# Attention scores as 64-row float32 product pairs, and another order of the input projections, in a two-layer hybrid block

## The chip, the cores and the metric

One core of one Trainium2 chip runs the whole two-layer block in one launch. The metric is the time of the launch on the device in microseconds; the median of the runs shown counts. The text names the engines as the profile does: PE multiplies matrices (PEld is its weight loading), DVE, ACT and POOL work element by element, SP issues the transfers.

## The reference

For 256 tokens of width 1024, each of two layers does `x = x + rms_norm(mixer(rms_norm(x)))` and then `x = x + rms_norm(swiglu(rms_norm(x)))`, all in float32. The mixer multiplies the normed input by a weight of 1024 x 6484 and cuts the product into the inputs of four branches:

```
ssm   (br 0): conv of xs, bs, cs (4 taps, silu), gate z, state-space scan, 8 heads
fox   (br 1): softmax(q k^T / 8 + cf_q - cf_k) v, causal, 8 heads of 64
moba  (br 2): softmax(rope(q) rope(k)^T / 8) v, causal (256 tokens are one block), 8 heads
dsa   (br 3): the same, over the 64 keys per query with the largest index score
              sum_h w_h relu(rope(iq_h) . rope(ik)), 4 index heads
out = (sum_n sigmoid(h Wg_n + b) * (y_n Wb_n)) Wo
```

## The kernel before

A weight matrix is worked off in **pieces**. A chunk of 1 MB is loaded by SP (three buffers, `raw`), and each half of it is split into a rounded part `whi` (ACT, line 307) and a rest `wlo` (DVE, line 123), 128x1024 each. A piece of a projection then is 24 PE matmuls of 256 columns: `hh*whi`, `hl*whi`, `hh*wlo` over 8 blocks of the input width (`emit_b`), where `hh` and `hl` are the split of the normed input. The splits run ahead of PE by constants: `HA = 3` pieces for `whi`, `LA = 2` for `wlo`. Some pieces (`mv`, `fv`, `dv`, the output projections) are 12 matmuls of 512 columns instead.

All other work is written as generators, and one step of each active one is emitted per **turn** (`tick`). The main loop emits, for each piece: the loads and splits ahead, the piece's matmuls, then one turn. Every engine executes in the order of emission. In a turn come first the `posts` (what follows a piece's matmuls, such as `rope_post`, `conv_post`, `z_post`), then the active generators, and then, if `STEP` turns have gone by since the last one, the next **unit** is taken from the list `units`. A unit is one pair of heads: `attn_gen` for the branches fox, moba and dsa (four units each), or `ssd_gen` for ssm (four). So there are 16 units per layer, in the order in which their projections are done. Here `STEP` is 3. `index_gen` computes the index scores (line 813), and then the top keys in 16 turns of a maximum and a replacement (lines 820 and 821), and sets the flag for which the dsa units wait.

A layer's mixer has 51 pieces of input projection in the order mv 4, fv 4, small 1, iq 2, mq 4, mk 4, xs 4, bs 2, cs 2, z 4, fq 4, fk 4, dv 4, dq 4, dk 4 (numbered 0 to 50 here). Then come four blocks of 12 pieces, one for each branch in the order 2, 0, 1, 3: in each, twice, four gate pieces and two projections of the branch's output `y`. The first projections are pieces 55, 67, 79 and 91. Before a projection `drain` gives further turns, with no piece between them, until the branch's last unit has set its flag.

An attention unit takes 14 turns: one for `split_k` (line 776 on ACT, 779 on DVE, 780 on POOL), one for `split_q` (764 on ACT, 767 on DVE), one to spare, then the steps score, low, expo, recip, norm, tr, ev for its two heads, one turn apart, then the product with v (`pv_mms`, all of 128 rows and 64 output columns, the two heads on separate halves of the columns), its rounding and its rest. The split puts the rounded q and its rest on top of each other as 128 rows, and k twice, so that `s_mms` gets a head's scores from one 128-row matmul with k's rounded part and one with k's rest (in zero-padded tiles `klz`), for each of two query tiles: 128 queries by 128 keys and 128 queries by 256 keys. Fox adds a third with the decay row (`csS`).

Of the kernel before, what the change touches and what calls it, by code (L numbers as in the profile page):

```python
# [15 lines left out]
P = 128  # L16
# [24 lines left out]
def host_constants():  # L41
    import numpy as np
    c = np.zeros((P, NCST), np.float32)
    p = np.arange(P)
    l = np.arange(S)
    c[:, C_ID:C_ID + P] = np.eye(P, dtype=np.float32)
    c[:, C_TRI:C_TRI + P] = p[:, None] <= p[None, :]
    c[:, C_ONE:C_ONE + P] = 1.0
    c[:, C_MASK:C_MASK + P] = np.where(p[None, :] > p[:, None], BIG, 0.0)
    c[:, C_MASK + P:C_MASK + 3 * P] = np.where(l[None, :] > p[:, None] + P, BIG, 0.0)  # L50
    c[:, C_MASKT:C_MASKT + P] = np.where(p[None, :] < p[:, None], -BIG, 0.0)
    inv = np.power(np.float32(10000.0), -np.arange(0, 64, 2, dtype=np.float32) / np.float32(64)).astype(np.float32)
    ang = (np.arange(S, dtype=np.float32)[:, None] * inv[None, :]).astype(np.float32)
    j = (p % 64) // 2
    c[:, C_COS:C_COS + S] = np.cos(ang).astype(np.float32)[:, j].T
    c[:, C_SIN:C_SIN + S] = np.sin(ang).astype(np.float32)[:, j].T * np.where(p % 2 == 0, -1.0, 1.0)[:, None]
    for r in range(16):
        c[r, C_SEL + r] = 1.0
        c[32 + r, C_SEL + r] = 1.0
    return c  # L60
# [2 lines left out]
NS4 = 26  # L63
TAIL = 6
MID = 1
STEP = 3
HA = 3
LA = 2

# [22 lines left out]
def kernel(ctx: ExitStack, tc: tile.TileContext, a, out):  # L92
# [68 lines left out]
    nh = cp.tile([P, 1], F32, name="nh")  # L161
    V.memset(nh, -0.5)
    csS = cp.tile([P, S], F32R, name="csS")
    klz = [cp.tile([P, 2, S], F32R, name=f"klz{i}") for i in range(2)]
    turn = [0]
    par = cp.tile([P, DEPTH, 76], F32, name="par")
    av = cp.tile([P, DEPTH, 16], F32, name="av")
    dsk = cp.tile([P, DEPTH, 4], F32, name="dsk")
# [13 lines left out]

    def clear_pads():
        G.memset(csS.bitcast(F32), 0.0)
        for z in klz:
            G.memset(z.bitcast(F32), 0.0)

    def setup_params():
        V.tensor_copy(sel, cst[:, C_SEL:C_SEL + 16])
        pp = aps()  # L190
        for l in range(DEPTH):
            T.transpose(pp[:, l * P:(l + 1) * P], rows[:, l, :], ident)
        pv = pp[:, 0:2 * P].rearrange("p (l c) -> p l c", l=DEPTH)
        V.tensor_scalar(par[:, :, 0:72], pv[:, :, 0:72], 0.5, None, op0=ALU.mult)
        V.tensor_copy(par[:, :, 72:76], pv[:, :, 72:76])
        V.memset(av, -1.0)
        for l in range(DEPTH):
            ea = tp.tile([P, 8], F32, name="ea")
            A.activation(ea, hd[:, l, 2, :], AF.Exp)
            V.tensor_scalar(av[:, l, 0:8], ea, -1.0, None, op0=ALU.mult)  # L200
            V.tensor_copy(dsk[0:64, l, :], hd[0:64, l, 3, 0:8:2])
            V.tensor_copy(dsk[64:128, l, :], hd[64:128, l, 3, 1:8:2])
# [309 lines left out]
    def mixer(l):  # L512
# [81 lines left out]
        def z_post(base):  # L594
            def f(j, o):
                i = base + j
                if i == 0:
                    L["sz"] = big("sz")
                zh = t1k("zh")
                A.activation(zh, o, AF.Copy, scale=0.5)  # L600
                yield from silu_half(zh, L["sz"][:, i, :])
                if i == 3:
                    L["y", 0] = (big("y0h", F32R), big("y0l", F32R))
                    for i in range(4):
                        units.append(ssd_gen(l, L, i))
            return f

        def bgemm(key, post, perm=False, n=4):
            for c in range(n // 2):
                add_b(cols_chunk(w, COL[key] + c * S, S, KT, perm), 2, post(2 * c))  # L610

        def agemm(key, first=False):
            cs, qs = add_a(w, [COL[key]], v_post(key), first and l > 0)
            if first:
# [3 lines left out]
                else:  # L618
                    qs[1].pre, qs[2].pre = st["t1"]

        agemm("mv", True)
        agemm("fv")
        add_b(small_chunk(w), 1, small_post)
        bgemm("iq", lambda b: rope_post("iq", b, lambda: start(index_gen(l, L)), 2), True, 2)
        bgemm("mq", lambda b: rope_post("mq", b), True)
        bgemm("mk", lambda b: rope_post("mk", b, start_attn(2, "mq", "mk", "mv")), True)
        bgemm("xs", conv_post)
        bgemm("bs", lambda b: conv_post(4 + b), n=2)
        bgemm("cs", lambda b: conv_post(6 + b), n=2)
        bgemm("z", z_post)  # L630
        bgemm("fq", fq_post)
        bgemm("fk", lambda b: fk_post(b, start_attn(1, "fq", "fk", "fv", fox=True)))
        agemm("dv")
        bgemm("dq", lambda b: rope_post("dq", b), True)
        bgemm("dk", lambda b: rope_post("dk", b, start_attn(3, "dq", "dk", "dv", dsa=True)), True)

        wg = a["w_gate"][l]

# [119 lines left out]

    HALVES = (LOWER, UPPER)

    def split_q(q, scale):
        qs = tp.tile([P, 2, S], F32R, name="qs", bufs=2)
        for b, h in enumerate(HALVES):
            A.activation(qs[h, b, :], q[h], AF.Copy, scale=scale)
        yield
        for b, h in enumerate(HALVES):
            V.scalar_tensor_tensor(qs[HALVES[1 - b], b, :], q[h], scale, qs[h, b, :].bitcast(F32),  # L767
                                   op0=ALU.mult, op1=ALU.subtract)
        return qs

    def split_k(k):
        kh = tp.tile([P, 2, S], F32R, name="kh", bufs=2)
        kl = klz[turn[0] % 2]
        turn[0] += 1
        for b, h in enumerate(HALVES):
            A.activation(kh[h, b, :], k[h], AF.Copy)
        yield
        for b, h in enumerate(HALVES):
            V.tensor_copy(kh[HALVES[1 - b], b, :], kh[h, b, :])
            G.tensor_tensor(kl[h, b, :], k[h], kh[h, b, :].bitcast(F32), op=ALU.subtract)  # L780
        return kh, kl

    def s_mms(ps, b, qs, kh, kl, bias=None):
        for sl, q0, n in QT:
            mm(ps[:, sl], qs[:, b, q0:q0 + P], kh[:, 0:n], True, False)
            mm(ps[:, sl], qs[:, b, q0:q0 + P], kl[:, 0:n], False, bias is None)
            if bias is not None:
                mm(ps[:, sl], selrow(bias), csS[:, 0:n], False, True)

    def index_gen(l, L):  # L790
        yield from wait(("w16", l))
        yield
        ikh = tp.tile([P, S], F32R, name="ikh")
        ikl = tp.tile([P, S], F32R, name="ikl")
        A.activation(ikh, L["ik"], AF.Copy)
        qs = [None, None]
        for i in range(2):
            qs[i] = yield from split_q(L["iq"][:, i, :], 1.0)
        sub_lo(ikl, L["ik"], ikh)
        yield  # L800
        acc = tp.tile([P, 384], F32, name="iacc")
        ps, rl = {}, {}
        for s in range(6):
            if s < 4:
                ps[s] = aps()
                s_mms(ps[s], s % 2, qs[s // 2], ikh, ikl)
            if 0 <= s - 1 < 4:
                rl[s - 1] = t15("irl")
                A.activation(rl[s - 1], ps[s - 1][:, :384], AF.Relu)
            h = s - 2  # L810
            if h >= 0:
                for t, (sl, q0, n) in enumerate(QT):
                    V.scalar_tensor_tensor(acc[:, sl], rl[h][:, sl], L["w16"][:, t, h:h + 1],  # L813
                                           mask[:, sl] if h == 0 else acc[:, sl],
                                           op0=ALU.mult, op1=ALU.subtract if h == 0 else ALU.add)
            yield
        for rnd in range(8):
            for t, (sl, q0, n) in enumerate(QT):
                m8 = tp.tile([P, 8], F32, name="m8", bufs=2)
                V.max(m8, acc[:, sl])  # L820
                V.match_replace(out=acc[:, sl], in_to_replace=m8, in_values=acc[:, sl], imm_value=DROP)  # L821
                yield
        L["dm"] = tp.tile([P, 384], F32, name="dm")
        V.tensor_scalar(L["dm"], acc, DROP * 0.5, BIG, op0=ALU.is_gt, op1=ALU.mult)
        V.tensor_tensor(L["dm"], L["dm"], mask, op=ALU.max)
        flags.add(("dm", l))

    def attn_gen(l, L, br, qk, kk, vk, i, fox, dsa):
        if fox:
            yield from wait(("cs", l))  # L830
        if dsa:
            yield from wait(("dm", l))
        kh, kl = yield from split_k(L[kk][:, i, :])
        qs = yield from split_q(L[qk][:, i, :], -0.125)
        yield
        v = L[vk]
        add = L["dm"] if dsa else mask
        ps, sm, mn, ls, rc, pr, pT, sT = ([None, None] for _ in range(8))

        def score(b):  # L840
            ps[b] = aps()
            s_mms(ps[b], b, qs, kh[:, b, :], kl[:, b, :], 8 + 2 * i + b if fox else None)

        def low(b):
            sm[b] = t15("sm")
            mn[b] = tp.tile([P, 2], F32, name="mn", bufs=4)
            for t, (sl, q0, n) in enumerate(QT):
                V.tensor_tensor_reduce(sm[b][:, sl], ps[b][:, sl], add[:, sl], op0=ALU.add, op1=ALU.min,  # L848
                                       scale=1.0, scalar=3e38, accum_out=mn[b][:, t:t + 1])

        def expo(b):
            pr[b] = tp.tile([P, 384], F32, name="pr", bufs=4)
# [332 lines left out]
```

## Time and profile before

| | us |
|---|---|
| median of 3 runs | 1130.69 |
| lowest, highest | 1130.31, 1187.93 |
| the profiled execution: time | 1132.14 |
| the profiled execution: span of the instructions | 1130.4 |

| engine | busy us | share of the span |
|---|---|---|
| PE | 1099.5 | 97% |
| PEld | 1031.5 | 91% |
| DVE | 767.1 | 68% |
| ACT | 631.2 | 56% |
| POOL | 277.8 | 25% |

Busy times are sums over the whole span; the stages differ. The ends of matmuls are modelled, so the time that one takes is read from its start to the start of the next. The chain that ended last gives PE 81%, DVE 13% and ACT 3% of the span. The granted clock (PEclk) is a share of 2.4 GHz, and its two levels are 1.2 and 2.4 GHz.

### The profile page before, as it was taken

To read this page: it belongs to the slowest core of one execution; us is meant where nothing else is said; L and a number is where in the kernel's file an instruction comes from. 1 tells how busy PE (TensorE), PEld (TensorE's weight loads), DVE (VectorE), ACT (ScalarE), POOL (GpSimd) and SP (SyncE) were. 2 spreads that over 40 slices of the span, in tenths; PEclk is the share of its full clock that TensorE was granted. 3 is DMA by queue.
4 is the path that set the end of the run, shared out by engine and by line. 5 is a ranking of instruction groups with operands and counts; after the bars stand their busy time and mean duration, and the time that the engine had idled before them with its cause. 6 is when DMAs were issued, how large, how long until landed. Compare 5 with 4: busy or idle time off the path is not lost.

```text
span 1130.4 us, 20409 instructions
## 1 busy us (share of the span) xinstructions
PE 1099.5 (97%) x8067; PEld 1031.5 (91%) x8067; DVE 767.1 (68%) x1430; ACT 631.2 (56%) x1190; POOL 277.8 (25%) x327
## 2 busy tenths in 40 slices
PE   7998999999999999999999979999999999999997
PEld 5997889999999799998879979899999988999986
DVE  6799969866547755546478999597754677545542
ACT  6646677676445554445355577757755455454531
POOL 1342337533222100000014424474331320000000
PEclk9998999999999999999999989999999999999999
DMA  7743443454557455556654435345446574565650
GB/s 225 227 150 112 150 149 119 155 163 146 162 191 242 138 185 181 186 188 224 224 141 133 150 112 175 125 135 165 125 155 196 183 238 150 179 195 165 220 194 37
DMA packets 153923, 188.96 MB, mean 167 GB/s; under 512 B 12740, under 2 KB 129764, under 8 KB 153828
## 3 DMA queue, kind: packets, MB, share of 16 engines
q1 hardware_dynamic: 153828, 187.67, 50.7%
q8 instruction: 63, 1.03, 0.4%
q14 instruction: 32, 0.26, 0.1%
HBM read 186.61 MB, written 1.05 MB: 166 GB/s over the span
## 4 chain that ended last, share of the span: by engine, by line
PE 81%; DVE 13%; ACT 3%; issue 2%; POOL 1%; DMA 0%; SPq 0%; DVEq 0%; POOLq 0%; ACTq 0%
PE g L120 61%; PE a L120 18%; DVE wlo L123 4%; DVE cacc L585 2%; PE a L870 2%; ACT junk L238 1%; DVE qs L767 1%; ACT whi L307 1%; DVE rsh L503 1%; POOL pnr L208 1%; DVE iacc L813 0%; DVE rt L504 0%; DVE ny L244 0%; DVE iacc L821 0%; DMA raw<-in_w_in_dram 0%
## 5 line engine op out<-in xcount | busy, mean ns | idle before, releaser
L123 DVE TENSOR_TENSOR wlo<-raw,whi 128x1024 fp32r<-128x1024 f32 (+2 forms) x386 | 444.2, 1170 | 106.6 <-ACT whi L307 84.7
L307 ACT ACTIVATE whi<-raw 128x1024 fp32r<-128x1024 f32 (+2 forms) x386 | 368.6, 986 | 63.9 <-DMA raw<-in_w_ffn_out_dram 37.9
L120 PE MATMUL g<-hh,whi 128*128 128x256 f32 x1776 | 254.9, 287 | 0.0
L120 PE MATMUL g<-hl,whi 128*128 128x256 f32 x1776 | 252.2, 285 | 0.0
L120 PE MATMUL g<-hh,wlo 128*128 128x256 f32 x1776 | 249.6, 283 | 0.0
L120 PEld LDWEIGHTS g<-hh,whi 128*128 128x128 f32 x1776 | 231.0, 193 | 1.3 <-issue 0.7
L120 PEld LDWEIGHTS g<-hl,whi 128*128 128x128 f32 x1776 | 232.1, 194 | 0.0
L120 PEld LDWEIGHTS g<-hh,wlo 128*128 128x128 f32 x1776 | 229.7, 192 | 0.0
L864 POOL TENSOR_SCALAR pr<-pr,rc 128x128 f32<-128x128 f32 x96 | 66.5, 705 | 132.7 <-DVE rc L860 119.0
L150 POOL TENSOR_SCALAR gain<-gain 128x1024 f32<-128x1024 f32 x4 | 4.8, 1207 | 335.6 <-DMA gain<-in_norm_ffn_post_dram 315.0
L643 ACT ACTIVATE gt<-g,par 128x256 f32<-128x256 f32 x64 | 30.3, 474 | 98.8 <-PE g L120 98.8
L663 POOL TENSOR_TENSOR mg<-mg,gt 128x256 f32<-128x256 f32 x48 | 53.5, 1123 | 112.6 <-DVE gt L657 112.6
L1017 DVE TENSOR_TENSOR hu<-gt,g 128x256 f32<-128x256 f32 x40 | 16.9, 421 | 87.0 <-PE g L120 87.0
L120 PE MATMUL a<-whi,hidh 128*128 128x512 f32 x176 | 55.6, 390 | 0.0
L120 PE MATMUL a<-wlo,hidh 128*128 128x512 f32 x176 | 55.5, 389 | 0.0
L120 PE MATMUL a<-whi,hidl 128*128 128x512 f32 x176 | 55.4, 389 | 0.0
L1009 ACT ACTIVATE gt<-g 128x256 f32<-128x256 f32 x40 | 15.4, 385 | 68.0 <-PE g L120 68.0
L506 POOL TENSOR_TENSOR rsh<-rsh,cst 128x256 f32<-128x256 f32 (+1 forms) x38 | 29.5, 777 | 89.3 <-DVE rsh L503 88.9
L657 DVE SCALAR_TENSOR_TENSOR gt<-gt,g 128x256 f32<-128x256 f32 x48 | 19.8, 419 | 40.0 <-PE g L120 34.0
L855 ACT ACTIVATE pr<-sm,mn 128x128 f32<-128x128 f32 x96 | 42.4, 446 | 3.4 <-DVE mn L848 3.4
L120 PE MATMUL g<-whi,hh 128*128 128x512 f32 x128 | 41.3, 404 | 1.6 <-ACT hh L278 1.0
L1019 ACT ACTIVATE hidh<-hu 128x256 fp32r<-128x256 f32 x40 | 16.7, 418 | 45.0 <-DVE hu L1017 45.0
(227 smaller groups left out, 1535.1 us busy)
## 6 DMA issues: line engine op xcount, KB each, us to landing
raw<-in_w_ffn_in_dram SPq DMA_DIRECT2D x40, 1024.0 KB, 5.1
raw<-in_w_in_dram SPq DMA_DIRECT2D x38, 1024.0 KB, 5.0
raw<-in_w_gate_dram SPq DMA_DIRECT2D x32, 1024.0 KB, 5.5
raw<-in_w_ffn_out_dram SPq DMA_DIRECT2D x22, 1024.0 KB, 4.9
raw<-in_w_branch_dram SPq DMA_DIRECT2D x16, 1024.0 KB, 5.0
raw<-in_w_in_dram SPq DMA_DIRECT2D x24, 512.0 KB, 6.3
raw<-in_w_out_dram SPq DMA_DIRECT2D x8, 1024.0 KB, 6.3
raw<-in_w_ffn_in_dram SPq DMA_DIRECT2D x8, 512.0 KB, 5.1
```

What stands on the lines that cost most here:

```text
L120: T.matmul(o, l, r, start=start, stop=stop)
L123: V.tensor_tensor(lo, src, hi.bitcast(F32), op=ALU.subtract)
L307: A.activation(dst(c.hi[i]), src(c.raw), AF.Copy)
L506: G.tensor_tensor(sh[:n], sh[:n], sin[:n], op=ALU.mult)
L585: V.scalar_tensor_tensor(ac[:, sft:], u[:, :S - sft], wcol(3 - sft), ac[:, sft:], op0=ALU.mult, op1=ALU.add)
L643: A.activation(th, o, AF.Tanh, bias=par[:, l, 40 + br * 8 + d:41 + br * 8 + d], scale=0.5)
L657: V.scalar_tensor_tensor(L["gt", d], L["gt", d], 1.0, os[j], op0=ALU.add, op1=ALU.mult)
L663: G.tensor_tensor(md, md, L["gt", d], op=ALU.add)
L855: A.activation(pr[b][:, sl], sm[b][:, sl], AF.Exp, bias=mn[b][:, t:t + 1], scale=-1.0, accum_out=ls[b][:, t:t + 1])
L864: G.tensor_scalar(pr[b][:, sl], pr[b][:, sl], rc[b][:, t:t + 1], 1.0, op0=ALU.mult, op1=ALU.mult)
L870: T.transpose(pT[b][:, js], pr[b][:, js], ident)
L1017: V.tensor_tensor(u, H["s", j], o, op=ALU.mult)
```

## The change

The rounding of q and k goes away (`split_q`, `split_k`, the tiles `qs`, `kh`, `klz`, `ikh`, `ikl`). Scores are float32 matmuls of 64 rows, the lower and the upper half of the rows one after the other into two banks, both heads in one step. The factor -0.125 moves into the reduction that adds the mask, and the signs and sizes of the mask, of `av` and of `dm` follow. The order of the pieces is now mv, fv, small, iq, mq, dv, mk, xs 2, fq 2, xs 2, fq 2, bs 2, fk 2, cs 2, z 4, fk 2, dq, dk. `index_gen` starts after the last z piece, not after iq. `STEP` is 4.

```diff
-    c[:, C_MASK:C_MASK + P] = np.where(p[None, :] > p[:, None], BIG, 0.0)
+    c[:, C_MASK:C_MASK + P] = np.where(p[None, :] > p[:, None], -8 * BIG, 0.0)
...
-STEP = 3
+STEP = 4
...
-        for z in klz:
-            G.memset(z.bitcast(F32), 0.0)
...
-        V.memset(av, -1.0)
+        V.memset(av, 8.0)
...
                 if i == 3:
+                    start(index_gen(l, L))
                     L["y", 0] = (big("y0h", F32R), big("y0l", F32R))
...
         agemm("mv", True)
         agemm("fv")
         add_b(small_chunk(w), 1, small_post)
-        bgemm("iq", lambda b: rope_post("iq", b, lambda: start(index_gen(l, L)), 2), True, 2)
...
+        bpair("iq", rope_of("iq", n=2), 0, True)
+        for c in range(2):
+            bpair("mq", rope_of("mq"), c, True)
         agemm("dv")
...
+        for c in range(2):
+            bpair("mk", mk, c, True)
+        bpair("xs", conv_of(0), 0)
+        bpair("fq", fq_post, 0)
+        bpair("xs", conv_of(0), 1)
+        bpair("fq", fq_post, 1)
+        bpair("bs", conv_of(4), 0)
+        bpair("fk", fk, 0)
+        bpair("cs", conv_of(6), 0)
+        bpair("z", z_post, 0)
+        bpair("z", z_post, 1)
+        bpair("fk", fk, 1)
...
-    def s_mms(ps, b, qs, kh, kl, bias=None):
-        for sl, q0, n in QT:
-            mm(ps[:, sl], qs[:, b, q0:q0 + P], kh[:, 0:n], True, False)
-            mm(ps[:, sl], qs[:, b, q0:q0 + P], kl[:, 0:n], False, bias is None)
-            if bias is not None:
-                mm(ps[:, sl], selrow(bias), csS[:, 0:n], False, True)
+    def scores(q, k, bias=None):
+        ps = [aps(), aps()]
+        for t, (sl, q0, n) in enumerate(QT):
+            for b, h in enumerate(HALVES):
+                mm(ps[b][:, sl], q[h, q0:q0 + P], k[h, 0:n], t == 0, t == 1 and bias is None)
+        if bias is not None:
+            for t, (sl, q0, n) in enumerate(QT):
+                for b in range(2):
+                    mm(ps[b][:, sl], selrow(bias + b), csS[:, 0:n], False, t == 1)
+        return ps
...
-        kh, kl = yield from split_k(L[kk][:, i, :])
-        qs = yield from split_q(L[qk][:, i, :], -0.125)
-        yield
...
         def score(b):
-            ps[b] = aps()
-            s_mms(ps[b], b, qs, kh[:, b, :], kl[:, b, :], 8 + 2 * i + b if fox else None)
+            if b == 0:
+                ps[:] = scores(L[qk][:, i, :], L[kk][:, i, :], 8 + 2 * i if fox else None)
```

## Rows read from the trace of the kernel before

**Rows 1.** The page, part 1: busy us, share of the span, instructions

```profile
PE 1099.5 (97%) x8067; PEld 1031.5 (91%) x8067; DVE 767.1 (68%) x1430; ACT 631.2 (56%) x1190; POOL 277.8 (25%) x327
```

**Rows 2.** Busy time by stretch: us, each engine (x instructions), PEclk, DMA share, GB/s

```profile
100.00:118.00 18.00, 12.64 (x88) 12.43 (x89) 17.33 (x51) 11.55 (x31) 4.68 (x6) 0.81 0.33 106
240.00:260.00 20.00, 20.00 (x171) 19.56 (x170) 13.09 (x37) 16.40 (x39) 7.33 (x12) 1.00 0.47 155
300.00:356.00 56.00, 56.00 (x469) 56.00 (x468) 31.33 (x36) 27.48 (x36) 17.46 (x15) 1.00 0.61 203
```

**Rows 3.** PE in time, layer 0: start, us, tiles, count, [idle before <-releaser]

```profile
97.13 1.12 PE L120 MATMUL g<-hh,wlo 128*128 128x256 f32 x8
103.48 0.44 PE L120 MATMUL a<-kh,qs 128*128 128x128 f32 x1 [5.22 <-DVE qs L767]
...
104.47 1.91 PE L120 MATMUL g<-hh,whi 128*128 128x256 f32 x8
...
108.82 0.22 PE L120 MATMUL a<-kh,qs 128*128 128x128 f32 x1
...
115.35 0.49 PE L870 MATMUL a<-cst,pr 128*128 128x128 f32 x3
117.73 0.33 PE L120 MATMUL a<-kh,qs 128*128 128x128 f32 x1 [1.88 <-DVE qs L767]
...
118.46 1.91 PE L120 MATMUL g<-hh,whi 128*128 128x256 f32 x8
...
122.66 0.22 PE L120 MATMUL a<-kh,qs 128*128 128x128 f32 x1
```

**Rows 4.** The same in layer 1

```profile
659.38 0.44 PE L120 MATMUL a<-kh,qs 128*128 128x128 f32 x1 [5.22 <-DVE qs L767]
...
673.62 0.33 PE L120 MATMUL a<-kh,qs 128*128 128x128 f32 x1 [1.67 <-DVE qs L767]
```

**Rows 5.** DVE by line, 59.97 to 122.66 us: count | busy us, mean ns | idle

```profile
L123 DVE TENSOR_TENSOR wlo<-raw,whi 128x1024 fp32r<-128x1024 f32 (+1 forms) x18 | 20.3, 1135 | 0.2
L585 DVE SCALAR_TENSOR_TENSOR cacc<-cu,par,cacc 128x255 f32<-128x255 f32 (+2 forms) x24 | 12.5, 522 | 0.6
L813 DVE SCALAR_TENSOR_TENSOR iacc<-irl,w,iacc 128x128 f32<-128x128 f32 (+1 forms) x6 | 4.2, 738 | 0.0
L767 DVE SCALAR_TENSOR_TENSOR qs<-iq,qs 64x256 fp32r<-64x256 f32 x4 | 3.2, 790 | 0.1
L820 DVE MAX8 m<-iacc 128x8 f32<-128x128 f32 (+1 forms) x8 | 2.8, 353 | 0.0
L821 DVE MATCH_REPLACE8 iacc<-m,iacc 128x128 f32<-128x128 f32 (+1 forms) x8 | 2.7, 342 | 0.0
L503 DVE STREAM_SHUFFLE rsh<-g 128x256 f32<-128x256 f32 x6 | 2.7, 448 | 0.0
L767 DVE SCALAR_TENSOR_TENSOR qs<-mq,qs 64x256 fp32r<-64x256 f32 x6 | 2.5, 420 | 0.2
L848 DVE CUSTOM_DVE_ANT_0 sm<-a,cst 128x128 f32<-128x128 f32 (+1 forms) x8 | 2.5, 349 | 0.0
...
L571 DVE SCALAR_TENSOR_TENSOR xsc<-th,cacc 128x256 f32<-128x256 f32 x4 | 2.2, 555 | 0.0
```

**Rows 6.** PE in time: float32 products of 128 rows, then the v product

```profile
123.12 1.47 PE L120 MATMUL a<-bc 128*128 128x256 f32 x8
124.35 1.20 PE L120 MATMUL g<-hh,whi 128*128 128x256 f32 x8
...
126.34 1.12 PE L120 MATMUL g<-hh,wlo 128*128 128x256 f32 x8
127.39 0.88 PE L120 MATMUL a<-sT,mv 128*64 128x256 f32 x8
128.20 0.55 PE L870 MATMUL a<-cst,pr 128*128 128x128 f32 x3
```

**Rows 7.** By line, whole span: weight loads of the scores' second product

```profile
L120 PEld LDWEIGHTS a<-klz,qs 128*128 128x128 f32 x96 | 19.0, 198 | 0.0
```

More of the change, by code (lines that the diff above doesn't have):

```diff
@@ L48, in host_constants @@
     c[:, C_ONE:C_ONE + P] = 1.0
-    c[:, C_MASK:C_MASK + P] = np.where(p[None, :] > p[:, None], BIG, 0.0)
-    c[:, C_MASK + P:C_MASK + 3 * P] = np.where(l[None, :] > p[:, None] + P, BIG, 0.0)
+    c[:, C_MASK:C_MASK + P] = np.where(p[None, :] > p[:, None], -8 * BIG, 0.0)
+    c[:, C_MASK + P:C_MASK + 3 * P] = np.where(l[None, :] > p[:, None] + P, -8 * BIG, 0.0)
     c[:, C_MASKT:C_MASKT + P] = np.where(p[None, :] < p[:, None], -BIG, 0.0)
@@ L163 @@
     csS = cp.tile([P, S], F32R, name="csS")
-    klz = [cp.tile([P, 2, S], F32R, name=f"klz{i}") for i in range(2)]
-    turn = [0]
     par = cp.tile([P, DEPTH, 76], F32, name="par")
@@ L606, in z_post, with bpair @@
             return f
-        def bgemm(key, post, perm=False, n=4):
-            for c in range(n // 2):
-                add_b(cols_chunk(w, COL[key] + c * S, S, KT, perm), 2, post(2 * c))
+        def bpair(key, post, c, perm=False):
+            add_b(cols_chunk(w, COL[key] + c * S, S, KT, perm), 2, post(2 * c))
         def agemm(key, first=False):
@@ L619, in agemm, with rope_of, conv_of @@
                     qs[1].pre, qs[2].pre = st["t1"]
+        def rope_of(key, last=None, n=4):
+            return lambda b: rope_post(key, b, last, n)
+        def conv_of(base):
+            return lambda b: conv_post(base + b)
+        fk = lambda b: fk_post(b, start_attn(1, "fq", "fk", "fv", fox=True))
+        dk = rope_of("dk", start_attn(3, "dq", "dk", "dv", dsa=True))
+        mk = rope_of("mk", start_attn(2, "mq", "mk", "mv"))
         agemm("mv", True)
@@ L623, in mixer @@
         add_b(small_chunk(w), 1, small_post)
-        bgemm("iq", lambda b: rope_post("iq", b, lambda: start(index_gen(l, L)), 2), True, 2)
[L625 to L632, printed above, removed]
-        agemm("dv")
-        bgemm("dq", lambda b: rope_post("dq", b), True)
-        bgemm("dk", lambda b: rope_post("dk", b, start_attn(3, "dq", "dk", "dv", dsa=True)), True)
+        bpair("iq", rope_of("iq", n=2), 0, True)
+        for c in range(2):
+            bpair("mq", rope_of("mq"), c, True)
+        agemm("dv")
+        for c in range(2):
[10 more added lines that the diff above has]
+        bpair("fk", fk, 1)
+        for c in range(2):
+            bpair("dq", rope_of("dq"), c, True)
+        for c in range(2):
+            bpair("dk", dk, c, True)
         wg = a["w_gate"][l]
@@ L759 @@
     HALVES = (LOWER, UPPER)
[L761 to L764, printed above, removed]
-        yield
[L766 to L781, printed above, removed]
-    def s_mms(ps, b, qs, kh, kl, bias=None):
-        for sl, q0, n in QT:
-            mm(ps[:, sl], qs[:, b, q0:q0 + P], kh[:, 0:n], True, False)
-            mm(ps[:, sl], qs[:, b, q0:q0 + P], kl[:, 0:n], False, bias is None)
-            if bias is not None:
-                mm(ps[:, sl], selrow(bias), csS[:, 0:n], False, True)
+    def scores(q, k, bias=None):
[8 more added lines that the diff above has]
+        return ps
     def index_gen(l, L):
         yield from wait(("w16", l))
[L792 to L799, printed above, removed]
         yield
@@ L803, in index_gen @@
         for s in range(6):
-            if s < 4:
-                ps[s] = aps()
-                s_mms(ps[s], s % 2, qs[s // 2], ikh, ikl)
+            if s in (0, 2):
+                ps[s], ps[s + 1] = scores(L["iq"][:, s // 2, :], L["ik"])
             if 0 <= s - 1 < 4:
@@ L814, in index_gen @@
                                            mask[:, sl] if h == 0 else acc[:, sl],
-                                           op0=ALU.mult, op1=ALU.subtract if h == 0 else ALU.add)
+                                           op0=ALU.mult, op1=ALU.add)
             yield
@@ L823, in index_gen @@
         L["dm"] = tp.tile([P, 384], F32, name="dm")
-        V.tensor_scalar(L["dm"], acc, DROP * 0.5, BIG, op0=ALU.is_gt, op1=ALU.mult)
-        V.tensor_tensor(L["dm"], L["dm"], mask, op=ALU.max)
+        V.tensor_scalar(L["dm"], acc, DROP * 0.5, -8 * BIG, op0=ALU.is_gt, op1=ALU.mult)
+        V.tensor_tensor(L["dm"], L["dm"], mask, op=ALU.min)
         flags.add(("dm", l))
@@ L832, in attn_gen @@
             yield from wait(("dm", l))
-        kh, kl = yield from split_k(L[kk][:, i, :])
-        qs = yield from split_q(L[qk][:, i, :], -0.125)
-        yield
         v = L[vk]
@@ L848, in low @@
                 V.tensor_tensor_reduce(sm[b][:, sl], ps[b][:, sl], add[:, sl], op0=ALU.add, op1=ALU.min,
-                                       scale=1.0, scalar=3e38, accum_out=mn[b][:, t:t + 1])
+                                       scale=-0.125, scalar=3e38, accum_out=mn[b][:, t:t + 1])
         def expo(b):
```

## The prediction

> **What bounds the kernel now.** I start with the busy shares [rows 1]. PE at 97% says that the kernel is PE's, but the ends of matmuls are modelled and a waiting PE can look busy, so I go on to the stretches [rows 2]. From 300 to 356 us PE starts 469 matmuls, one per 0.119 us, with nothing in between: there a piece of 24 takes 24 x 0.12 = 2.88 us, and PE alone sets the pace. From 240 to 260 us attention units run beside the gate pieces, DVE is busy 13.09 of 20 us, and PE still never stops. From 100 to 118 us the picture turns: DVE is busy 17.33 of 18 us, PE starts only 88 matmuls, and the granted clock averages 0.81. ACT (11.55) and DMA (share 0.33) have room there. So DVE is the bound in that stretch.
>
> PE in time shows what that costs [rows 3]. The last eight matmuls before it start at 97.13 and are through at 97.13 + 8 x 0.12 = 98.09; the next one, a score product, starts at 103.48, released by DVE's `qs`. That is 5.39 us. PE then runs slow: the first head's four score matmuls take 103.48 to 104.47, 0.99 us against the 0.46 of an undisturbed head (122.66 [rows 3] to 123.12 [rows 6]), which is 0.53 more, and the piece behind takes 104.47 to 108.82, 4.35 against 2.88, 1.47 more. At 115.35 three transposes start (0.11 each, a 128-column pass being a twelfth of the 1.23 us in [rows 6], so through at 115.68), and the next score waits for `qs` until 117.73: 2.05 us. Its four matmuls cost 0.73 - 0.46 = 0.27 more, its piece (118.46 to 122.66) 4.20 - 2.88 = 1.32 more. Sum 5.39 + 0.53 + 1.47 + 2.05 + 0.27 + 1.32 = **11.0 us**. Layer 1 shows the same two waits, 5.22 and 1.67 us instead of 5.22 and 1.88 [rows 4], so 10.8 us. Together **21.8 us**. Elsewhere in the mixers PE's own matmuls fill its time.
>
> **What DVE loses, and gets elsewhere.** From 59.97 to 122.66 us, sixteen pieces (mk, xs, bs, cs, z), DVE's groups are listed [rows 5]. The splits of mq and its k go: `qs<-mq` 2.5 us and the casts of k at line 779, which I price as the same (same shape, about 6), an upper bound of 5 us for both. The index moves out, later: `qs<-iq` 3.2 (this one vanishes), the sums 4.2 and more for the first head, the maxima 2.8, the replacements 2.7, so 12.9 us. Of 62.7 us that leaves some 45. The eight convolution pieces (three taps of 0.522 and a gate of 0.555 each, 2.1 us) are no longer in a row.
>
> Counted for the new order, the sixteen pieces from xs to z's second: 16 `wlo` x 1.135 = 18.2; 24 taps, 12.5; ten gates x 0.555, 5.6; four units, each four `sm` x 0.349 and an estimated 1.1 for sums, reciprocals and the rest of y, 10.0. **46 us on DVE.** PE needs 16 x 2.88 = 46.1, and per unit scores 0.92, six transposes 0.66 and the v product 0.90, 4 x 2.5: **56 us**. DVE has 10 us to spare, so both waits go. I take all **-21.8**; the ends are half of it (-11) and all.
>
> The next stretch is tighter. In the eight dq and dk pieces DVE has 8 x (1.135 + two rope operations of 0.45) = 16.3, the index sums (eight of 0.74, 5.9), a first maximum and replacement (0.7), two ssm units and the scaling of x by dt (estimated 4): 27 us, against 23.0 for PE's pieces, 1.84 for index scores and about 3 for ssm, 28. It just fits, with two pieces of `wlo` ahead. I add **+1** for both layers, ends 0 and 8.
>
> **The scores on PE.** Per pair of heads: before, eight 128-row matmuls, 2 x 0.46 = 0.92 us. After, four float32 products, each executed as two passes, so again eight. The trace has no 64-row product; two rows bound it. Eight such passes of the same lengths with 128 rows, in series (`bc`), take 123.12 to 124.35 = 1.23 us [rows 6]. The v product is also eight passes of these lengths, on two halves of the columns: from the end of the piece before it (126.34 + 0.96 = 127.30) to the next operation at 128.20 it takes **0.90** us [rows 6], though half of 1.23 would be 0.62; the 0.28 is the change of shape on both sides. So: 0.62 if pairs overlap and the change is free; 0.90 as in the v product; 0.92 + 0.28 = 1.20 if pairs overlap but loads of 128 columns bind as in the old scores (the v product's have 64); 1.23 + 0.28 = 1.51 if nothing overlaps. I take **1.0**, nearest to the v product and a little towards the loads. There are 28 pairs (24 units, two index pairs per layer): 28 x 0.08 = **+2.2**, ends -8.4 and +16.5. Fox's decay products stay the same in number.
>
> One rule of the Trainium skill speaks against the overlap: "TensorE: Matmul & The Clock Gate", Part 3 (what overlaps and what doesn't) has matmuls start and end in strict program order. The four products come as lower, upper, lower, upper, two passes each, so by it only neighbouring passes would overlap. The trace disagrees: the v product is emitted head after head, and in order would take 11 of the 12 units of `bc`'s 1.23 us, 1.13, where its starts span 0.81 [rows 6].
>
> **Turns.** The spread of units over turns is where I see a new cost. Before, units start every 3 turns, the last dsa unit in turn 66; it ends in turn 79, long before piece 91 wants it, and `drain` never turns. After, moba starts at 25, 29, 33, 37, ssm (after z) at 43, 47, 51, 55, fox at 59 to 71, dsa to 87. An ssm unit with the norm of its group needs 15 turns after its start: the last is done in turn 70, but piece 67 asks when 67 turns have gone, so `drain` adds **3 turns**. A dsa unit now needs 10 turns: done in 97, with piece 91 asking at 94, **3 more**. The same in layer 1. In these turns nothing of a piece covers a unit's steps. In the first, PE has a v product (0.90) and a fox pair's scores (about 1.5) to run while DVE and ACT normalise and split y, each behind other work in its queue; the projection waits for the rest. Bounds: nothing, or a stall like the second one of layer 0 with its slow clock, 2.05 + 0.27 + 1.32 = 3.64 [rows 3]. I take 2.5. The second needs only a copy and a subtraction after the v product: 1.0, same ends. Two layers: 2 x 3.5 = **+7**, ends 0 and +14.6.
>
> **At no cost:** what leaves ACT and POOL (both under DVE in every stretch); the larger mask; the loads, which keep their sizes (DMA share 0.33 to 0.61 [rows 2]); dv's early place. On SP's queue only the order of 1 MB chunks changes, one per two pieces as before; on ACT the eight index activations and the copies of fq, fk and dv come at other pieces, under 2.88 us of PE each, and if ACT fell behind there, a late `whi` would show as a wait of DVE. The wait of the dsa units for the top keys is met in turn 66, before they start at 75.
>
> **Sum:** -21.8 + 1 + 2.2 + 7 = -11.6. The profiled execution took 1132.14, 1.45 above the median of 1130.69; 1132.1 - 11.6 - 1.45 = **1119 us**.
>
> **Rivals.**
> - *No overlap of the halves*, 1.51 a pair: +14.3 against my 1.0, **1133**. For it: no 64-row pair was ever seen here. Against: the column halves do overlap [rows 6]. 0.13.
> - *Strict order* (the skill's rule, as a mechanism here): eight units of `bc`'s twelve, 0.82 + 0.28 = 1.10 a pair, +2.8, **1122**. The rows above speak against it. 0.07.
> - *DVE binds again at dq and dk*, where rope, index sums and ssm meet: 4 us a layer, 7 more than I take, **1126**. 0.10.
> - *Everything goes well*: pairs at 0.80, drains free, no wait at dq: -21.8 - 3.4, **1106**, faster by more than 2%. 0.09.
> - *Slower*: in the 64-row shape a pass's weights can't load while the other half multiplies. Each of eight loads then stands in the open with its 0.198 us [rows 7]: 1.51 + 1.58 = 3.1 a pair, 28 x 2.1 = +59, **1178**. It decides from about 2.2 us a pair. Against: the v product's loads are hidden. 0.04.
>
> My forecast keeps 0.57. The range runs from the good case to the case without overlap, 1105 to 1134; outside lie the slow rival and the tails of both ends, under 2 in 10. A measurement of this kernel tells about 2% from no change, 1108 to 1153: faster 0.10, same 0.86, slower 0.04.
>
> **What would show it.** Right: no wait of PE for DVE between xs and z, PEclk 1.00 there; a pair's eight passes in 0.8 to 1.2 us, lower and upper starting close together; a gap of 1 to 4 us ahead of the first projections of branches 0 and 3, and nowhere else. Wrong: passes of one pair in series; a wait for `wlo` or `iacc` during dq and dk; a granted clock below 1.00 after a drain, which would make it dearer than I take.

## The result, and the profile after

The changed kernel takes **1116.72 us** (median of 4 runs, 1114.72 to 1118.67); the kernel before, run beside it, 1130.5. The ratio is 0.9882, with an interval of 0.9858 to 0.9906: 13.8 us faster, and by less than the 2% that this measurement tells from no change. Two of its four executions took 1114.7 and 1115.1 us at a mean granted clock of 0.998 and more, the other two, the profiled one among them, 1118.4 and 1118.7 at 0.994 and 0.995. The forecast was 1119 in a range of 1105 to 1134. The total came out 2 us from it, but two terms of the sum were wrong, with opposite signs, and the experiments below are mainly about them.

The profiled execution took 1118.67 us (span 1116.7). The page's part 1, which answers to [rows 1], and the first row of its part 4, the shares of the chain that ended last:

```profile
PE 1096.8 (98%) x8067; PEld 1017.3 (91%) x8067; DVE 717.2 (64%) x1324; ACT 587.4 (53%) x1084; POOL 239.6 (21%) x277
...
PE 88%; DVE 5%; ACT 2%; DMA 1%; issue 1%; POOL 1%; SPq 1%; DVEq 0%; POOLq 0%; ACTq 0%
```

PE has as many instructions as before. DVE lost 50 us of work, but the row that matters is the chain: DVE's share fell from 13% to 5%, PE's rose from 81% to 88%. The stretches tell where. First one of the kernel before that reaches from mk to the second wait, then those of the kernel after (us, busy time and instructions of each engine, PEclk, DMA share, GB/s):

```profile
88.00:122.00 34.00, 26.81 (x192) 26.19 (x192) 32.89 (x84) 23.69 (x59) 8.14 (x9) 0.85 0.36 118
```

```profile
60.00:66.00 6.00, 6.00 (x16) 4.84 (x17) 5.94 (x11) 3.50 (x6) 3.22 (x3) 0.50 0.43 140
88.00:152.00 64.00, 64.00 (x535) 61.00 (x534) 45.83 (x102) 45.59 (x106) 12.99 (x17) 1.00 0.52 165
85.62:139.06 53.44, 53.44 (x450) 50.98 (x449) 40.95 (x92) 35.11 (x82) 11.21 (x15) 1.00 0.52 166
152.00:190.00 38.00, 38.00 (x318) 35.76 (x317) 33.99 (x71) 20.41 (x41) 20.32 (x23) 1.00 0.37 116
```

Between xs and z PE now starts a matmul every 64/535 = 0.120 us and never stops; DVE has 18 us to spare in 64. The third row is the time in which PE works off the sixteen pieces that the prediction counted. The fourth is the stretch of dq and dk: DVE is busy 34 of 38 us, and PE still runs through. The first row is new: six microseconds at half clock, 16 matmuls. What is in front of it stands in the waits of PE for DVE (us in total, times, longest):

```profile
PE a L268 <- DVE ny L240: 3.5, 3, 2.2
PE a L120 <- DVE sg L748: 3.2, 2, 2.4
PE g L120 <- DVE y0l L123: 1.0, 2, 0.5
```

The four waits for `qs` are gone. The wait for `sg`, the small series on DVE that `gates_gen` needs (softplus of the ssm steps and of fox's decay), was one of 0.7 us before; it is two now, 2.4 us of it in layer 0. PE there, with starts, durations and the idle time ahead:

```profile
54.91 1.12 PE L120 MATMUL g<-hh,wlo 128*128 128x256 f32 x8
58.43 0.83 PE L120 MATMUL a<-cst,sg 128*16 128x128 f32 x6 [2.40 <-DVE sg L748]
59.19 1.38 PE L120 MATMUL a<-sg,cst 128*128 128x16 f32 x6
60.41 1.20 PE L120 MATMUL g<-whi,hh 128*128 128x512 f32 x2
...
65.67 0.85 PE L120 MATMUL g<-whi,hh 128*128 128x512 f32 x2
...
68.66 0.62 PE L120 MATMUL g<-whi,hh 128*128 128x512 f32 x2
...
71.38 0.62 PE L120 MATMUL g<-whi,hh 128*128 128x512 f32 x2
```

After the wait the first dv piece takes 60.41 to 65.67, 5.26 us; the third, at full clock, takes 68.66 to 71.38, 2.72. So in this execution the wait costs twice: 2.40, and 2.54 of slow clock in that piece alone. DVE in the same time, before and after:

```profile
51.64 2.30 DVE L123 TENSOR_TENSOR wlo<-raw,whi 128x512 fp32r<-128x512 f32 x2
...
54.53 0.64 DVE L726 TENSOR_SCALAR sg<-sg 128x32 f32<-128x32 f32 x1
...
58.28 0.19 DVE L735 TENSOR_TENSOR sg<-sg,av 128x32 f32<-128x32 f32 x1
```

```profile
50.48 3.36 DVE L123 TENSOR_TENSOR wlo<-raw,whi 128x1024 fp32r<-128x1024 f32 x2
...
54.44 0.64 DVE L739 TENSOR_SCALAR sg<-sg 128x32 f32<-128x32 f32 x1
...
58.18 0.19 DVE L748 TENSOR_TENSOR sg<-sg,av 128x32 f32<-128x32 f32 x1
```

Ahead of the series before stood the split of one mq piece, in two halves, 2.30 us. Now it is the splits of two dv pieces, 3.36: 1.06 more. PE was through with the piece ahead at 54.91 + 0.96 = 55.87, 1.8 us sooner than in the execution before (gained before 21 us, where that execution waited longer and then ran at the lower clock), but the series ended only 0.1 us sooner. With the same place of dv the wait of layer 0 was 1.8 us in four of the kernels below, and 3.0 and 3.1 in two; in the two below with the old order of pieces it was 0.7 ("index late") and too short to be listed ("scores alone").

The scores of a moba pair, and the matmuls around them:

```profile
90.42 1.12 PE L120 MATMUL g<-hh,wlo 128*128 128x256 f32 x8
91.47 0.93 PE L120 MATMUL a<-mk,mq 64*128 64x128 f32 x8
92.32 1.22 PE L120 MATMUL g<-hh,whi 128*128 128x256 f32 x8
...
95.30 1.12 PE L120 MATMUL g<-hh,whi 128*128 128x256 f32 x8
```

The eight passes take 92.32 - 91.47 = 0.85 us, as in all 28 pairs (0.85 or 0.86). The eight matmuls before them end at 90.42 + 0.96 = 91.38, so 0.09 is lost going in; the piece behind takes 95.30 - 92.32 = 2.98 instead of 2.88, 0.10 going out. Together **1.04 us**, against 0.92 for a pair before.

Last the turns of `drain` ahead of piece 67, where I had expected a stall of 2.5 us:

```profile
237.61 0.60 PE L120 MATMUL a<-cst,srs 128*128 128x128 f32 x4
238.15 0.88 PE L120 MATMUL a<-sT,fv 128*64 128x256 f32 x8
238.96 0.93 PE L120 MATMUL a<-fk,fq 64*128 64x128 f32 x8
239.81 0.73 PE L120 MATMUL a<-csS,sel 128*128 128x128 f32 x4
240.38 0.82 PE L853 MATMUL a<-cst,pr 128*128 128x128 f32 x6
240.95 0.72 PE L120 MATMUL g<-y0h,whi 128*128 128x256 f32 x4
241.51 0.40 PE L120 MATMUL g<-y0l,whi 128*128 128x256 f32 x2
242.38 0.72 PE L120 MATMUL g<-y0l,whi 128*128 128x256 f32 x2 [0.47 <-DVE y0l L123]
```

The units in flight give PE matmuls without a gap from 237.61 to 241.75, and the one wait is 0.47 us. Ahead of piece 91 the projection follows the last v product by 0.80 us (325.70 to 326.50), with no wait.

### The profile page after: what moved, and what is told of

It reads as the page before. It is cut to its first block, busy times and chain, and to the rows that moved or that the text cites. A ratio compares the mean times of both kernels' runs of the same rounds, so it can differ in the third digit from the quotient of the medians.

```text
span 1116.7 us, 20081 instructions
## 1 busy us (share of the span) xinstructions
PE 1096.8 (98%) x8067; PEld 1017.3 (91%) x8067; DVE 717.2 (64%) x1324; ACT 587.4 (53%) x1084; POOL 239.6 (21%) x277
## 4 chain that ended last, share of the span: by engine, by line
PE 88%; DVE 5%; ACT 2%; DMA 1%; issue 1%; POOL 1%; SPq 1%; DVEq 0%; POOLq 0%; ACTq 0%
PE g L120 68%; PE a L120 19%; DVE wlo L123 2%; DMA raw<-in_w_in_dram 1%; PE a L853 1%; ACT whi L303 1%; ACT junk L234 1%; POOL pnr L204 1%; SPq L294 0%; DVE ny L240 0%; DVE hl L123 0%; DVE rsh L499 0%; DVE x L226 0%; DVE sg L745 0%; DVE rt L500 0%
## 5 line engine op out<-in xcount | busy, mean ns | idle before, releaser
L123 DVE TENSOR_TENSOR wlo<-raw,whi 128x1024 fp32r<-128x1024 f32 (+2 forms) x386 | 449.9, 1185 | 106.1 <-ACT whi L303 84.7
L120 PE MATMUL g<-hl,whi 128*128 128x256 f32 x1776 | 249.3, 283 | 0.0
L120 PEld LDWEIGHTS g<-hh,whi 128*128 128x128 f32 x1776 | 227.9, 191 | 6.7 <-issue 3.7
L120 PEld LDWEIGHTS g<-hl,whi 128*128 128x128 f32 x1776 | 229.0, 192 | 0.0
L847 POOL TENSOR_SCALAR pr<-pr,rc 128x128 f32<-128x128 f32 x96 | 63.7, 674 | 142.1 <-DVE rc L843 142.1
L676 POOL TENSOR_TENSOR mg<-mg,gt 128x256 f32<-128x256 f32 x48 | 50.1, 1050 | 93.2 <-DVE gt L670 90.1
L120 PE MATMUL g<-wlo,hh 128*128 128x512 f32 x128 | 41.1, 403 | 0.8 <-DVE wlo L123 0.8
L120 PE MATMUL g<-whi,hl 128*128 128x512 f32 x128 | 41.2, 404 | 0.6 <-DVE hl L276 0.6
```

The costliest lines, as they stand in the source:

```text
L120: T.matmul(o, l, r, start=start, stop=stop)
L123: V.tensor_tensor(lo, src, hi.bitcast(F32), op=ALU.subtract)
L676: G.tensor_tensor(md, md, L["gt", d], op=ALU.add)
L847: G.tensor_scalar(pr[b][:, sl], pr[b][:, sl], rc[b][:, t:t + 1], 1.0, op0=ALU.mult, op1=ALU.mult)
```

## The experiments

Each was timed beside the kernel before (1131.4 to 1131.5 there). "After" is the changed kernel.

**Scores alone.** The after, with the pieces in the old order, `index_gen` behind iq, and `STEP` 3.

```diff
-STEP = 4
+STEP = 3
...
-                    start(index_gen(l, L))
...
-        bpair("xs", conv_of(0), 0)
-        bpair("fq", fq_post, 0)
...
+        bgemm("iq", lambda b: rope_post("iq", b, lambda: start(index_gen(l, L)), 2), True, 2)
...
+        bgemm("xs", conv_post)
```

> The kernel before with the new scores alone: 64-row float32 pairs from unsplit q and k, but the old order of pieces, the index scores from iq on, a unit every 3 turns. Theory A (the two waits of PE for DVE, 21.8 us in all, come from too much DVE work between mk and z, and the splits are a fifth of it while the index search is the larger part): the score step no longer waits for a split, but DVE still lags there, so PE waits for wlo or for probabilities instead; a third to two thirds of the 21.8 us come back, and the pairs cost 28 x 0.1 = 3 us: 1114 to 1126 us. Rival B (the splits of q and k alone made the wait): all 21.8 us come back: about 1112 us, PE without a wait for DVE between mk and z.

1117.15 us, ratio 0.9867 (0.9852 to 0.9883). The stretch of the convolutions is still DVE's, and the wait has another name:

```profile
88.00:122.00 34.00, 31.87 (x247) 29.28 (x246) 33.26 (x97) 23.35 (x59) 12.16 (x12) 0.95 0.42 126
```

```profile
108.86 0.48 PE L120 MATMUL a<-mk,mq 64*128 64x128 f32 x2
111.48 1.64 PE L120 MATMUL a<-mk,mq 64*128 64x128 f32 x6 [2.13 <-DVE mn L826]
```

DVE is busy 33.26 of 34 us. Without splits PE no longer waits for `qs`; it waits for `low` of an earlier head to free the bank into which the next scores go, 2.13 us, and the clock falls behind it (0.95 over the stretch). Less work for DVE takes most of the loss away, not all.

**Order alone.** The kernel before with the new order and the later index; q and k split, `STEP` 3.

```diff
+                    start(index_gen(l, L))
...
-        bgemm("xs", conv_post)
-        bgemm("bs", lambda b: conv_post(4 + b), n=2)
...
+        bpair("xs", conv_of(0), 0)
+        bpair("fq", fq_post, 0)
+        bpair("xs", conv_of(0), 1)
```

> The new order alone: pieces in the new order and the index scores after z, but q and k still split, two 128-row products per head, a unit every 3 turns. Theory A (order and place of the index search are what clears DVE): DVE's count for the 16 pieces from xs to z is 46 + 4 x 1.75 = 53 us against 56 for PE, so both waits go, no drains, no dearer pairs: 1107 to 1113 us. Rival B (the splits made the wait): a wait of PE for qs stays, of several us per layer: 1120 us or more.

1111.62 us, ratio 0.9827 (0.9812 to 0.9842): faster than the after, whose interval begins at 0.9858.

```profile
88.00:152.00 64.00, 64.00 (x537) 62.58 (x536) 53.36 (x118) 52.27 (x122) 22.52 (x24) 1.00 0.54 165
```

DVE still makes the splits (53.36 us against 45.83 in the after), and PE runs through all the same. So the order needs no help from the scores to remove both waits.

**Index late.** The kernel before, with only `index_gen` started after the last z piece.

```diff
                 if i == 3:
+                    start(index_gen(l, L))
...
-        bgemm("iq", lambda b: rope_post("iq", b, lambda: start(index_gen(l, L)), 2), True, 2)
+        bgemm("iq", lambda b: rope_post("iq", b, None, 2), True, 2)
```

> The kernel before with one move: the index search starts after the last z piece instead of after iq; old order of pieces, split q and k, a unit every 3 turns. Theory A (the index search is the larger part of the excess on DVE between mk and z: it takes 13 us and more out of about 66 in a stretch of 63): the waits shrink to a third or less, 1110 to 1117 us. Rival B (the eight convolution pieces in a row are what DVE can't follow, with or without the search): at least half of the wait stays, 1120 us or more.

1117.09 us, 0.9872 (0.9856 to 0.9889). DVE in the stretch goes on at 32.69 of 34 us, but PE now starts 269 matmuls there, not 192. The first row is the stretch; the next two are PE's largest waits for DVE beside those of the norms:

```profile
88.00:122.00 34.00, 32.22 (x269) 31.45 (x269) 32.69 (x84) 29.01 (x75) 13.01 (x16) 1.00 0.48 155
```

```profile
PE a L120 <- DVE qs L768: 3.1, 2, 1.8
PE g L120 <- DVE mg L655: 2.3, 2, 1.1
```

The waits for `qs` are 3.1 us instead of 14.0 (the four of [rows 3, 4]).

**Index early.** "Order alone", with the index back behind iq.

```diff
-                    start(index_gen(l, L))
...
-        bpair("iq", rope_of("iq", n=2), 0, True)
+        bpair("iq", rope_of("iq", lambda: start(index_gen(l, L)), 2), 0, True)
```

> The new order of the pieces with split q and k and a unit every 3 turns, but the index search from iq on, as before. Theory A (either the spread of the convolution pieces or the later search is enough, since each takes DVE's excess of a few us off the stretch): 1110 to 1115 us, near the 1111.6 of the new order with the late search. Rival B (the search has to leave the stretch): a wait of PE for DVE between mk and z stays, 1118 us or more.

1120.91 us, 0.9904 (0.9886 to 0.9922): 9.3 us slower than with the late index.

```profile
88.00:140.00 52.00, 49.93 (x415) 48.84 (x414) 50.38 (x130) 37.87 (x87) 18.87 (x20) 1.00 0.45 144
```

```profile
PE a L120 <- DVE qs L787: 4.1, 6, 0.8
```

The spread alone leaves DVE at 50.38 of 52 us, and Rival B holds. The loss between mk and z comes in six waits, 4.1 us in all, each of at most 0.8 us, behind which the clock stays at 1.00, rather than in two of 5 and 2 us a layer, behind which it fell [rows 2]. Not all of the 9.3 us is the index search: this profiled execution also ran at the lower clock behind its wait of 1.83 us for `sg`, and the one of "order alone" did not, behind 1.79:

```profile
60.00:66.00 6.00, 6.00 (x20) 4.69 (x19) 5.84 (x11) 3.04 (x5) 2.67 (x4) 0.50 0.08 17
```

**Step 3.** The after, units every three turns, so that `drain` has nothing to do.

```diff
-STEP = 4
+STEP = 3
```

> The changed kernel with a unit every 3 turns instead of 4: by the count of turns no drain is left in either layer. Theory A (the six drain turns of a layer cost about 1.3 us as the trace after shows: a slow first projection of branches 0 and 3): 2 to 3 us faster than the changed kernel, 1112 to 1115. Rival B (the wider spread of units was needed, since DVE lags again where units start every 3 turns): waits of PE for DVE come back, and it is slower than the changed kernel by 3 us or more. The forecast on record put the drains at 7 us, by which this would be at 1110.

1115.13 us, 0.9858 (0.9841 to 0.9875). By the medians the drains of the after cost 1116.72 - 1115.13 = 1.6 us, less than the 2 to 3 of Theory A; the intervals overlap, so it may be nothing. The waits of Rival B do not come back. From "order alone", run beside it, this kernel differs by the scores alone: 1115.13 - 1111.62 = 3.5 us by the medians, 2.5 between the profiled executions (1114.26 and 1111.79). 28 pairs x (1.04 - 0.92) would be 3.4: the new scores cost PE time.

**Step 5.** The after with more drains: 19 turns of `drain` in a layer instead of 6.

```diff
-STEP = 4
+STEP = 5
```

> The changed kernel with a unit every 5 turns: by the count of turns the drains of a layer grow from 6 turns to 19 (8, 3 and 8), ahead of the first projections of branches 0, 1 and 3. Theory A (a drain turn costs PE only what other units' steps don't fill, and in a long drain there is little of them: 0.5 to 1 us a turn): 13 more turns in each of two layers, 13 to 26 us slower than the changed kernel: 1129 to 1142. Rival B (drains are hidden whatever their length, as a unit every 3 turns against 4 made no difference): within 3 us of the changed kernel.

1125.27 us, 0.9949 (0.9935 to 0.9963): 26 more turns for 8.6 us more than the after, 0.33 a turn. That is between the two theories, and neither holds. The rows are from ahead of piece 67:

```profile
234.72 0.94 PE L120 MATMUL a<-cst,ysq 128*128 128x128 f32 x6 [0.65 <-ACT ysq L945]
...
239.99 0.89 PE L853 MATMUL a<-cst,pr 128*128 128x128 f32 x3 [0.73 <-POOL pr L847]
...
242.23 0.64 PE L120 MATMUL g<-y0h,whi 128*128 128x256 f32 x4
```

In a run of empty turns only some wait, and by less than a microsecond each. My 2.5 us for three turns was taken from a wait of another kind.

**Heads apart.** The after, the scores of each head of a pair in a turn of their own.

```diff
-            for b, h in enumerate(HALVES):
-                mm(ps[b][:, sl], q[h, q0:q0 + P], k[h, 0:n], t == 0, t == 1 and bias is None)
+            mm(ps[:, sl], q[h, q0:q0 + P], k[h, 0:n], t == 0, t == 1 and bias is None)
...
-            if b == 0:
-                ps[:] = scores(L[qk][:, i, :], L[kk][:, i, :], 8 + 2 * i if fox else None)
+            ps[b] = scores(L[qk][:, i, :], L[kk][:, i, :], b, 8 + 2 * i if fox else None)
```

> The changed kernel with each head's scores emitted in a turn of its own, so that lower and upper rows can't overlap. Theory A (the two halves of the rows overlap, and each change of shape costs about 0.4 us on both sides together): a head then takes half of 1.23 us and 0.4 more, 1.0 us, a pair 2.0 against the 1.03 read from the trace after: 28 x 1.0 = 28 us slower than the changed kernel at most, 1135 to 1146. Rival B (no overlap even now, the 64-row products are short by themselves): no change but the second change of shape, 28 x 0.4 = 11 us: about 1128.

1140.87 us, 1.0091 (1.0067 to 1.0114), slower than the kernel before.

```profile
92.15 0.92 PE L120 MATMUL a<-mk,mq 64*128 64x128 f32 x4
93.00 1.22 PE L120 MATMUL g<-hh,whi 128*128 128x256 f32 x8
```

The four passes of one head take 0.85 us, as long as the eight of a pair: the second head of a pair costs nothing. Without pairing the kernel is 1140.87 - 1116.72 = 24 us slower.

**Head by head.** The after, the four products emitted lower, lower, upper, upper.

```diff
-        for t, (sl, q0, n) in enumerate(QT):
-            for b, h in enumerate(HALVES):
+        for b, h in enumerate(HALVES):
+            for t, (sl, q0, n) in enumerate(QT):
```

> The changed kernel with the four float32 products of a pair emitted head after head (lower 128, lower 256, upper 128, upper 256) instead of alternating. Theory A (passes on other rows are started ahead of earlier ones that wait for theirs, as the product with v shows on the columns): no change, within 2 us of the changed kernel, a pair still about 1.03 us. Rival B (matmuls start strictly in program order): only the upper head's first pass overlaps the lower's last, a pair's passes take 11 units of 0.1025 instead of 6, so 0.5 us more, 28 x 0.5 = 14 us slower than the changed kernel: about 1130.

1116.3 us, 0.9866 (0.9851 to 0.9881), as the after.

```profile
91.81 0.93 PE L120 MATMUL a<-mk,mq 64*128 64x128 f32 x8
92.67 1.22 PE L120 MATMUL g<-hh,whi 128*128 128x256 f32 x8
```

0.86 us instead of 0.85. The trace has the starts of the eight passes in pairs, 0.013 us apart, at 91.81, 92.03, 92.14 and 92.36, where a head alone in "heads apart" has single starts at the same distances (92.15, 92.36, 92.47 and 92.69). So the halves overlap in both orders of emission: a matmul of the upper half starts though earlier ones of the lower half have not started. That every engine executes in the order of emission, as said of the kernel before, does not hold for the two halves on PE.

**Gates one turn later.** The after, with one more turn in `gates_gen` ahead of the matmuls that take `sg`.

```diff
         L["dt"] = sp
         yield
+        yield
         pc = aps()
```

> The changed kernel with one more turn between the small gates' series on DVE and the cumulative sums on PE that wait for it. In the trace after, PE waits there for sg for 2.4 us in layer 0 and 0.8 in layer 1, and the profiled execution ran the two pieces behind the first wait at half clock. Theory A (dv's early place put two wlo of 1.7 us ahead of the series on DVE, and PE has nothing else in that turn): the wait goes, 2 to 3 us faster than the changed kernel, and up to 6 against its slower executions: 1110 to 1114. Rival B (DVE is late there as such, the next matmul would wait for dv's wlo instead): no change, 1115 to 1118.

1111.5 us, 0.9823 (0.9809 to 0.9836): 5.2 us less than the after, with intervals apart. The waits for `sg` are gone, and so is the slow stretch:

```profile
60.00:66.00 6.00, 6.00 (x28) 4.96 (x28) 5.94 (x10) 2.58 (x5) 3.19 (x3) 1.00 0.42 133
```

28 matmuls instead of 16, at a clock of 1.00 instead of 0.50. The line takes away the whole wait, also the 0.7 us that the kernel before had.

**Order, and gates later.** "Order alone" with the same line: the old scores, the new order, the later index.

```diff
         L["dt"] = sp
         yield
+        yield
         pc = aps()
```

> The best part so far, the new order alone with split q and k and a unit every 3 turns (1111.6 us), with the extra turn ahead of the cumulative sums. Theory A: its waits for sg, 1.8 and 0.7 us, go: 1108 to 1110 us, which would beat both kernels. Rival B: no change, 1111 to 1112 us.

**1107.88 us**, 0.9795 (0.9781 to 0.9808), against 0.9827 without the line. It beats both kernels: 8.8 us under the after, 23.6 under the kernel before it was run with.

## Why the prediction came out right, step by step

| step | predicted, us | measured, us | by |
|---|---|---|---|
| both waits of each layer go | -21.8 | gone | no wait of PE from mk to z |
| dq and dk | +1 | 0 | 38.00 of 38 us busy, no wait |
| score pairs | +2.2 (1.0 each) | +3.5 (1.04 each) | step 3 against order alone |
| `drain` | +7 | 0 to 1.6 | step 3 against the after |
| dv's early place | 0 | +4.5 at most | gates one turn later: 5.2, less the 0.7 of waiting that was there before |
| sum | -11.6 | -13.8 to -12.2; whole kernel -13.8 | with -21.8 for the waits |

The mechanism of the largest term held. That the total came within 2.3 us is luck: the drains were 5.4 to 7 us too dear, and dv's place, at nothing, some 4.5 too cheap.

**The waits.** The place, the bound and the size held: [rows 3] and [rows 4] give 21.8 as the sum of what goes, and "order, and gates later", with neither wait, no drain and the old scores, is 23.6 us faster than the kernel before, 0.7 of it the old wait for `sg`. The count of DVE's work was high: 46 us, where DVE is busy 40.95 in the 53.44 us of those sixteen pieces, and PE's 56 was high with it. What I did not see is that the parts are not additive. Scores alone, index alone and order with index late each give 14 to 20 us, because each takes a different piece from the same overload of DVE. Once the order had removed the waits, the scores had nothing left to gain, and cost about 3 us.

**The score pairs.** The mechanism held, the size was near: 0.85, plus 0.19 on the two sides, 1.04, for which I had taken 1.0. My parts were off: 0.62 for the passes leaves 0.42 for all else, where I had read 0.28 off the v product [rows 6]. About half of it lies inside the 0.85: ahead of the second pass, which starts 0.21 us after the first where the third starts 0.11 after the second, and ahead of the next shape. Adding the second half is free. The rival without overlap (1.51 a pair) falls with "heads apart", the slow one (3.1 a pair) with the 0.85 itself.

**Strict order** falls with "head by head". Its price, 1.10 a pair, is close to the 1.04 measured, so the size alone wouldn't have told; that order makes no difference does. The Trainium skill, "TensorE: Matmul & The Clock Gate", Part 3 (what overlaps and what doesn't), has matmuls start and end in program order; these runs disagree on the starts, as four passes of the lower half emitted first take no longer with the upper half's behind them, 0.86 us, and the upper half's start beside them.

**The drains** were the first failed step, "I take 2.5" and "1.0, same ends". The turns are there (both heads' transposes stand in one row at 240.38), but I priced them by the wait for `qs`, in which PE had nothing. In a drain the units in flight have matmuls of their own, and these must run somewhere: 237.61 to 241.75 is work brought forward, not a stall. The gap of 1 to 4 us that the prediction named as a sign of being right is not there.

**"dv's early place"**, costed at nothing, was the second. The paragraph looked at SP's queue and at `whi`, and not at what is queued behind dv's splits on DVE: the small series for the gates, for which PE waits two pieces later. That wait was 0.7 us before, which "elsewhere in the mixers PE's own matmuls fill its time" had passed over. So the series had no slack, and the 1.06 us put ahead of it on DVE went to PE: 0.73 + 1.06 = 1.8, the wait in four kernels. Why it was 2.4 to 3.1 in three others with the same place of dv stays open, and no run moved dv alone. In some executions the wait was paid a second time through the clock.

Left open: up to 1.6 us between the sum and the measured -13.8, which is within the spread of the runs.

## What to carry to other kernels

When a piece is moved, list for each engine what stands behind its first instructions in the queue, the smallest chains above all: a short series that was already a little late can cost more than a large one with slack. When two parts of a change both relieve one engine, price the second on the kernel that has the first; here the order of the pieces with the later index did it, and the cheaper scores on DVE were dearer on PE. Price empty turns by what PE still has to run in them, not by the worst wait of the trace.

## What was not expected of the hardware

A head alone, four float32 passes of 64 rows, takes 0.85 us, and a second one on the other half of the rows takes 0.85 with it, in both orders of emission that were run. So these 64-row products are only worth it in pairs.

A wait of 2.4 us of PE, after some 30 us of matmuls without a gap, was followed by six microseconds at the lower clock level (0.50, that is 1.2 GHz, from 60 to 66 us); the waits of up to 0.8 us in "index early" left it at 1.00. It fell behind 3.1 us in "head by head" and 3.0 in "step 5" too. In between, the length of the wait does not decide: behind 1.8 us for the same `sg` the clock fell in "index early", and stayed at 1.00 in "order alone", "step 3" and "heads apart".

The split of one piece on DVE took 2.30 us at 51.64 in the kernel before, while POOL worked from 51.49, and 1.31 a little earlier, while POOL was idle. The rows are DVE's and POOL's in the kernel before:

```profile
49.73 1.31 DVE L123 TENSOR_TENSOR wlo<-raw,whi 128x512 fp32r<-128x512 f32 x2
```

```profile
48.99 0.77 POOL L508 TENSOR_TENSOR iq<-rt,rsh 128x256 f32<-128x256 f32 x1
51.49 0.74 POOL L506 TENSOR_TENSOR rsh<-rsh,cst 128x256 f32<-128x256 f32 x1 [1.74 <-DVE rsh L503]
52.31 1.08 POOL L508 TENSOR_TENSOR mq<-rt,rsh 128x256 f32<-128x256 f32 x1
```

The whole trace of the kernel before says the same: the 42 splits of this shape with POOL idle all took 0.68 to 0.71 us, and the 28 with POOL at work for more than half of their time 1.07 on average, 1.24 at most. So a split is slow only beside POOL there. No run here changed that alone, and it is a reading, not a test.
